# One global order for a decoder layer: the same instructions put out along one table over all engines

## The chip, the cores and the metric

The kernel runs on one core of one Trainium2 chip. The metric is the device time of one execution in microseconds; the median of three runs before the change is 768.79 us (768.78 to 768.81). A core has a tensor engine (PE) for matmuls, a vector engine (DVE), a scalar engine (ACT), GpSimd (POOL) and a sync engine (SP) that here only issues transfers. Each engine takes its instructions in the order in which they stand in its queue; semaphores hold an instruction until what it needs is there.

## The reference, cut to what matters

The layer has 512 tokens of width 1024. Three gated branches read the same normed input; two norms of the result and a feed-forward network (FFN) of width 2816 follow.

```python
u = rms_norm(h, ln_mix_pre[l])
qa, ka, va, qb, kb, vb, qm, gl = jnp.split(jnp.einsum('bsd,de->bse', u, w_in[l]), split_idx, axis=-1)
y_swa = swa_sink_attention(qa, ka, va, swa_sinks[l], rel_bias)   # 8 heads of 64, window 128
y_sb  = stick_breaking_attention(qb, kb, vb)                     # 8 heads of 64, causal
y_mem = memory_cross_attention(qm, mk, mv)                       # 4 heads of 128, memory of 256
g = jax.nn.sigmoid(gl.reshape(B, S, N_BRANCH, D))
merged = (g[:, :, 0] * (y_swa @ w_branch_swa) + g[:, :, 1] * (y_sb @ w_branch_sb)
          + g[:, :, 2] * (y_mem @ w_branch_mem))
h = h + rms_norm(merged @ w_out[l], ln_mix_post[l])
u = rms_norm(h, ln_ffn_pre[l])
h = h + rms_norm((jax.nn.silu(u @ w_gate[l]) * (u @ w_up[l])) @ w_down[l], ln_ffn_post[l])
```

(The heads' reshapes are left out here, and the einsums of the branches are written as products.)

## The kernel before

**Arithmetic.** All large products are f32 made of three float32r matmuls. ACT makes `hi`, a float32r copy of a tile (CAST in the profile), DVE makes `lo = raw - hi` (TENSOR_TENSOR `lo<-raw,hi`), and PE does hi by hi, hi by lo and lo by hi (`mm3`). Weights come in pieces of 128 by 1024 into four places `raw`, and are split into four places `hi` and four `lo`. The gate and branch products and the FFN are computed as seven products of half-size blocks in place of eight, with sums and differences on DVE.

**Stages by time.** From 0 to about 90 us the projections of the three attentions, with the mean square of x (`rstd_of`) and of the memory; from 90 to about 225 us stick-breaking and window attention, with the memory's attention and parts of the gates between; to about 370 us gates and branch products; then the product with `w_out`, the second norm, and from about 450 us the FFN, the last of it `w_down` and the output.

**The reciprocal root of x.** `rstd_of("x", ...)` sums squares over the partitions with two matmuls against ones (`sh_x` and `sl_x` are the two halves of the sum of squares); `rsqrt` then does Ln on ACT (`t_x<-bank,eps_t`), Exp on ACT (`wide<-t_x`), and one Newton step of three DVE instructions (`t_x<-wide`, `t_x<-t_x,v_x`, `wide<-t_x,wide`). Only with it can DVE empty the banks of the projections of keys and queries (`kb<-bank,wide`, `qb<-bank,wide`). `table(name)` asks for a table of functions on ACT (ACT_TABLE_LOAD in the profile); the first such call stands ahead of the first activation. `eps_t` is one column filled by a DVE MEMSET.

**Value products of 64 columns.** `sb_out` multiplies the attention weights of two heads (`at`) by the values (in `wide`), for key blocks 3, 2, 1 and 0, with 512, 384, 256 and 128 elements; the inner loop runs over the two heads, whose results lie in the two halves of one PSUM bank. These are plain f32 matmuls with 64 columns of weights. The window attention does the same with `pts`, 256, 256, 256 and 128 elements. Transposes go through PE against the identity `c_ident`.

**Order and places.** Every engine is wrapped by `Noted`, which calls the real engine at once and keeps the instruction (its call is line 232, so nearly all instructions bear that line in the profile). The program is thus put out in the order of the code. At the end of `tile_kernel` a table of five lists, one for each engine, gives the order that each engine is to keep: `follow` ties each instruction to the one ahead of it in its list. The lists are independent of each other. `Places` hands out the places of tiles by a second table, `PLAN`, in the order in which the code asks for them. Helpers for runs without tables (`after`, `behind`, `high_priority`) stand in the code as well.

Of the kernel before, what the change touches and what calls it, by code (L numbers as in the profile page):

```python
# [17 lines left out]
P = 128  # L18
# [19 lines left out]
ORDER = {  # L38
    "tensor": (
# [23 lines left out]
    ),  # L63
    "vector": (
# [81 lines left out]
    ),  # L146
}
PLAN = {
    "raw": (
# [2042 lines left out]
```

## Time and profile before

| what | value |
|---|---|
| median of 3 runs | 768.79 us (768.78 to 768.81) |
| span of the profiled execution, first to last instruction | 766.9 us |
| granted clock of PE, mean | 0.997 |
| PE busy | 759.1 us, 99%, 4073 matmul records |
| DVE busy | 675.2 us, 88%, 1100 |
| ACT busy | 520.3 us, 68%, 946 |
| POOL busy | 104.1 us, 14%, 140 |
| moved by DMA | 150.06 MB, mean 196 GB/s |

For the profiled execution the span alone is recorded; the median stands 1.9 us above it, which lies ahead of the first and behind the last instruction.

How rows of a timeline are read: start in us, duration in us, engine, line, operation, `out<-in` by the program's names with their numbers left out, partitions by elements, type, and how many instructions of one kind stand in the row; in brackets the idle time ahead and what ended it. For a matmul `128*64 128x512` means weights of 128 rows and 64 columns and a moving operand of 128 partitions by 512 elements. The record of a matmul includes its way through the array, so consecutive records overlap; the pitch from start to start is what a matmul costs in a row of them. Rows by stage give the stretch, its length, and then for PE, PE's weight loads, DVE, ACT and POOL the busy time with the count of instructions; behind them the clock, the DMA share and GB/s. A row of a group gives the busy time, the mean ns of one, and the idle time ahead with what ended it.

### The profile page before, as it was taken

Reading aid. Unit: us, or ns where it says so; the run is one execution under the profiler, and the core shown is the slowest. Engines: PE = TensorE matmul, PEld = TensorE weight load, DVE = VectorE, ACT = ScalarE, POOL = GpSimd, SP = SyncE. Lnnn points to the kernel's source line nnn. Section 1 sums busy time; section 2 is a strip of 40 time slices with the busy share of each in tenths; the row PEclk is TensorE's granted clock in tenths of the full one; section 3 lists DMA queues with packets and bytes.
Section 4 is the critical chain, followed back from the end, with each engine's and each line's share of the span. In section 5 each row is a group of like instructions: output and inputs, shape, how many; then the busy total and the mean of one; then the engine's idle time right before and its main releaser. Section 6 shows DMA issues by size and latency. Waiting matters only on the chain.

```text
span 766.9 us, 11497 instructions
## 1 busy us (share of the span) xinstructions
PE 759.1 (99%) x4073; PEld 647.3 (84%) x4073; DVE 675.2 (88%) x1100; ACT 520.3 (68%) x946; POOL 104.1 (14%) x140
## 2 busy tenths in 40 slices
PE   9999999999999999999999999999999999999996
PEld 6789888778888888888888899988888888888885
DVE  7994897799989756999897799899999999999966
ACT  7662677777997758677944596566666668957552
POOL 0303242000222110010001201100000000214000
PEclk9999999999999999999999999999999999999998
DMA  8548999734799895469949958876777746859922
GB/s 277 166 142 233 332 328 254 211 111 149 185 188 192 184 203 163 112 134 210 340 128 329 209 130 240 203 191 180 204 192 203 220 142 187 171 120 216 261 75 111
DMA packets 50170, 150.06 MB, mean 196 GB/s; under 512 B 5984, under 2 KB 7952, under 8 KB 50016
## 3 DMA queue, kind: packets, MB, share of 16 engines
q1 hardware_dynamic: 34224, 94.38, 36.8%
q0 software_dynamic: 15600, 54.80, 36.1%
q8 instruction: 32, 0.52, 0.3%
q14 instruction: 26, 0.21, 0.1%
q10 hardware_dynamic: 288, 0.13, 0.1%
HBM read 140.38 MB, written 19.40 MB: 208 GB/s over the span
## 4 chain that ended last, share of the span: by engine, by line
PE 96%; DMA 1%; DVE 1%; ACT 1%; issue 0%; SPq 0%; DVEq 0%
PE bank L232 96%; DMA xT<-in_xT 1%; DMA raw<-in_w_p 0%; DVE xacc L232 0%; SPq L232 0%; ACT pair L232 0%; DVE pair L232 0%; ACT hi L232 0%; ACT xT L232 0%; DVE lo L232 0%; DVE fg L232 0%; DVE sl_x L232 0%; DVEq L2180 0%; DVE s L232 0%; ACT sqr L232 0%
## 5 line engine op out<-in xcount | busy, mean ns | idle before, releaser
L232 PE MATMUL bank<-pair,hi 128*128 128x512 f32 (+1 forms) x1008 | 254.4, 368 | 0.0
L232 DVE TENSOR_TENSOR lo<-raw,hi 128x1024 fp32r<-128x1024 f32 (+4 forms) x149 | 170.7, 1149 | 36.8 <-ACT hi L232 36.2
L232 PEld LDWEIGHTS bank<-pair,hi 128*128 128x128 f32 x1008 | 177.5, 189 | 27.0 <-ACT hi L232 0.9
L232 ACT CAST hi<-raw 128x1024 fp32r<-128x1024 f32 (+4 forms) x149 | 147.7, 998 | 73.7 <-PE bank L232 54.5
L232 PE MATMUL bank<-hi,pair 128*128 128x512 f32 (+1 forms) x628 | 196.3, 374 | 0.0
L232 PE MATMUL bank<-pair,lo 128*128 128x256 f32 (+1 forms) x752 | 154.7, 302 | 0.0
L232 PEld LDWEIGHTS bank<-hi,pair 128*128 128x128 f32 x628 | 115.3, 188 | 19.5 <-issue 0.2
L232 PEld LDWEIGHTS bank<-pair,lo 128*128 128x128 f32 x752 | 115.6, 190 | 10.9 <-DVE lo L232 0.7
L232 PE MATMUL bank<-lo,pair 128*128 128x512 f32 (+1 forms) x330 | 123.6, 375 | 0.0
L232 ACT CAST hi<-wide 128x1024 fp32r<-128x1024 f32 (+1 forms) x61 | 62.2, 1024 | 27.0 <-PE bank L232 11.3
L232 DVE TENSOR_TENSOR lo<-wide,hi 128x1024 fp32r<-128x1024 f32 (+1 forms) x61 | 71.9, 1185 | 4.6 <-ACT hi L232 4.3
L232 PEld LDWEIGHTS bank<-lo,pair 128*128 128x128 f32 x330 | 62.0, 188 | 10.1
L232 POOL DMA_DIRECT2D raw<-in_w_g x24 | 21.1, 878 | 124.4 <-DVE lo L232 106.2
L232 DVE TENSOR_TENSOR gp<-gp,bank 128x512 f32<-128x512 f32 x49 | 33.6, 687 | 4.6 <-PE bank L232 3.7
L232 ACT ACTIVATE sg<-gp 128x256 f32<-128x256 f32 x42 | 17.7, 421 | 23.0 <-DVE gp L232 22.9
L232 POOL DMA_DIRECT2D raw<-in_w_gu x15 | 13.2, 924 | 147.6 <-DMA raw<-in_w_gu 138.5
L232 ACT COPY gp<-bank 128x512 f32<-128x512 f32 x42 | 24.7, 588 | 2.1 <-DVE aq L232 1.4
L232 DVE TENSOR_TENSOR_SCAN bw<-br,bw 128x512 f32<-128x512 f32 (+3 forms) x32 | 24.6, 809 | 0.2
L232 DVE TENSOR_TENSOR gp<-gp,hp 128x512 f32<-128x512 f32 x36 | 24.7, 685 | 0.0
L232 POOL DMA_DIRECT2D wide<-in_w_gu x12 | 11.2, 934 | 84.6 <-DMA wide<-in_w_gu 76.3
L232 ACT COPY hp<-bank 128x512 f32<-128x512 f32 x36 | 21.5, 598 | 0.0
L232 PE MATMUL bank<-hi,ll 128*128 128x512 f32 x50 | 19.4, 389 | 0.0
(624 smaller groups left out, 1371.8 us busy)
## 6 DMA issues: line engine op xcount, KB each, us to landing
wide<-in_w_gu SPq DMA_DIRECT2D x31, 512.0 KB, 5.1
raw<-in_w_gu SPq DMA_DIRECT2D x26, 512.0 KB, 5.4
raw<-in_w_g POOLq DMA_DIRECT2D x24, 512.0 KB, 6.0
raw<-in_w_g SPq DMA_DIRECT2D x18, 512.0 KB, 4.2
raw<-in_w_gu POOLq DMA_DIRECT2D x15, 512.0 KB, 7.2
raw<-in_w_p SPq DMA_DIRECT2D x14, 512.0 KB, 6.3
wide<-in_w_gu POOLq DMA_DIRECT2D x12, 512.0 KB, 5.8
raw<-in_w_brt SPq DMA_DIRECT2D x9, 512.0 KB, 4.8
```

What stands on the lines that cost most here:

```text
L232: ins = f(*args, **kw)
```

## The change

All calls to engines are first noted as `Op` in a `Program`: nothing is put out, and nothing is allocated. Tiles out of `PLAN` that need an allocation are `View`s made `once`, when the first instruction that uses them is put out. At the end one table `ORDER` over all 6328 operations (4009 for PE, 1068 for DVE, 876 for ACT, 136 for POOL, 239 for SP, the same operations in the same noted order as before) says in which order they are put out; each is tied to the one ahead of it on its own engine. Both tables are new: of PE's 4009 operations 2996 keep their order among themselves, of DVE's 1068 546, of ACT's 876 420, of POOL's 136 94 and of SP's 239 141. `PLAN` gives other places to the tiles. The helpers for runs without tables are gone. The only order that is still asserted is that an activation comes behind the call for its table.

```diff
-ORDER = {
-    "tensor": (
-        "0-18 21 19-20 22-24 27 25-26 28-529 538-561 572-575 580-588 642 562-564 566-567 576-579 530-537 613-620 569 "
...
-class Noted:
...
-            ins = f(*args, **kw)
-            self.seen.append(ins)
-            return ins
+ORDER = (
+    "3 1 13 630 15 18 4 12 632 263 16 5 17 631 6 19 267 7 20 299 21 8 23 37 9 303 25 38 10 22 335 39-40 11 26 339 "
...
+class Program:
+    def __init__(self):
+        self.ops = []
+
+    def put_out(self, nc, order, follow):
+        real = lambda x: x.real() if isinstance(x, View) else x
+        last, out = {}, set()
+        for n in order or range(len(self.ops)):
+            op = self.ops[n]
+            assert all(b.at in out for b in op.behind)
+            out.add(n)
+            args = [real(x) for x in op.args]
+            ins = getattr(getattr(nc, op.engine), op.name)(*args, **{k: real(x) for k, x in op.kw.items()})
+            if op.engine in last:
+                follow(ins, last[op.engine])
+            last[op.engine] = ins
...
 class Places:
...
         if kind == "ck" and n < SINGLES:
-            return pool.tile(shape, dt, tag=f"ck{n}", name=name, bufs=1)
+            return View(once(lambda: pool.tile(shape, dt, tag=f"ck{n}", name=name, bufs=1)))
...
     def table(name):
         ins = nc.scalar.preload_act_table_set(name)
-        for x in since:
-            after(ins, x)
+        ins.behind = tuple(since)
         since.clear()
         pin[:] = [ins]
...
     go(len(fs.units))
-    for e, text in ORDER.items():
-        seen, last = getattr(nc, e).seen, None
-        for part in text.split():
-            a, _, b = part.partition("-")
-            for k in range(int(a), int(b or a) + 1):
-                if last is not None:
-                    follow(seen[k], seen[last])
-                last = k
+    order = []
+    for part in ORDER.split():
+        a, _, b = part.partition("-")
+        order += range(int(a), int(b or a) + 1)
+    program.put_out(tc.nc, order, follow)
```

Three places show what moves. The rows give the line (232 before, 425 after, both the helper), the operation, and the tiles by name and number.

PE before, the first value products of stick-breaking attention, heads 0 and 1 (`at0...` and `at1...`); `mh` and `hi` behind them belong to the memory's keys:

```order
L232 MATMUL bank0_104<-kbs11_326,qbl11_456 128x256
L232 MATMUL bank0_104<-at10_1039,wide0_84 64x512
L232 MATMUL bank0_104<-at00_951,wide0_84 64x512
L232 MATMUL bank0_104<-at11_1040,wide0_84 64x384
L232 MATMUL bank0_104<-at01_952,wide0_84 64x384
L232 MATMUL bank0_104<-at12_1041,wide0_84 64x256
L232 MATMUL bank0_104<-at02_953,wide0_84 64x256
L232 MATMUL bank0_104<-at12_1041,wide0_84 64x128
L232 MATMUL bank0_104<-at02_953,wide0_84 64x128
L232 MATMUL bank0_104<-mh0_734,hi0_76 128x256
```

All eight groups of such products stand like this before. PE after, the third group, heads 4 and 5:

```order
L425 MATMUL bank0_101<-pair5_107,hi3_79 128x512
L425 MATMUL bank0_101<-at50_1447,wide0_84 64x512
L425 MATMUL bank0_101<-hi2_78,ml3_516 128x512
```
```order
L425 MATMUL bank0_101<-pair8_110,hi3_79 128x512
L425 MATMUL bank0_101<-at40_1404,wide0_84 64x512
L425 MATMUL bank0_101<-at51_1451,wide0_84 64x384
L425 MATMUL bank0_101<-at41_1392,wide0_84 64x384
L425 MATMUL bank0_101<-at52_1438,wide0_84 64x256
L425 MATMUL bank0_101<-c_ident_118,bw60_1455 128x128
L425 MATMUL bank0_101<-at42_1388,wide0_84 64x256
L425 MATMUL bank0_101<-at52_1438,wide0_84 64x128
L425 MATMUL bank0_101<-at42_1388,wide0_84 64x128
L425 MATMUL bank0_101<-pair2_104,pair3_105 128x512
```

`at50` now stands some ten matmuls ahead of its partner `at40`, and a transpose stands inside the rest. The 64 products stand in 20 unbroken runs in place of 8; the sizes of the runs are 1 and 7 (heads 0 and 1), 2, 3, 1 and 2 (2 and 3), 1, 4 and 3 (4 and 5), 2, 4 and 2 (6 and 7); then for the window's four pairs 7 and 1, 8, 5 and 3, and 1, 4 and 3. Transposes against `c_ident` stand in 57 runs in place of 42.

ACT before, around the root of x (`t_x` is Ln, `wide<-t_x` is Exp; its first table load is the third row of its queue, far ahead of these):

```order
L232 CAST sh_x_298<-xacc_203 128x512
L232 CAST hi0_76<-raw0_72 128x1024
L232 CAST hi1_77<-raw1_73 128x1024
L232 ACTIVATE t_x_305<-bank0_104,eps_t_119 128x512
L232 CAST hi2_78<-raw2_74 128x1024
L232 ACTIVATE wide0_84<-t_x_305 128x512
L232 CAST hi3_79<-raw3_75 128x1024
L232 CAST kbs00_316<-kb0_295 64x512
```

ACT after, the same place (`pair13<-xacc` is what `sh_x` was):

```order
L425 CAST pair13_115<-xacc_191 128x512
L425 CAST hi0_76<-raw1_73 128x1024
L425 CAST hi2_78<-raw2_74 128x1024
L425 CAST hi1_77<-raw0_72 128x1024
L425 CAST hi3_79<-raw3_75 128x1024
L425 CAST hi0_76<-raw1_73 128x960
L425 ACTIVATE mh0_431<-mT0_254,wide0_84 128x256
L425 ACT_TABLE_LOAD
L425 ACTIVATE t_x_440<-bank0_101,eps_t_116 128x512
L425 ACT_TABLE_LOAD
L425 ACTIVATE wide0_84<-t_x_440 128x512
```

Ln and Exp now come behind three more CASTs, and a table load stands ahead of each. In the table the call for the combined table comes behind both; the loads are put in as the program is built, which has 12 of them in place of 9. DVE after, the same place:

```order
L425 TENSOR_TENSOR lo3_83<-raw3_75,hi3_79 128x1024
L425 TENSOR_TENSOR lo0_80<-raw1_73,hi0_76 128x960
L425 MEMSET eps_t_116 128x1
L425 SCALAR_TENSOR_TENSOR t_x_440<-wide0_84 128x512
L425 SCALAR_TENSOR_TENSOR ml0_456<-mT0_254,wide0_84,mh0_431 128x256
L425 TENSOR_TENSOR t_x_440<-t_x_440,v_x_356 128x512
L425 SCALAR_TENSOR_TENSOR wide0_84<-t_x_440,wide0_84 128x512
L425 SCALAR_TENSOR_TENSOR ml1_472<-mT1_269,wide0_84,mh1_463 128x256
L425 SCALAR_TENSOR_TENSOR kb1_476<-bank0_101,wide0_84 128x512
L425 SCALAR_TENSOR_TENSOR kb2_482<-bank0_101,wide0_84 128x512
L425 SCALAR_TENSOR_TENSOR kb3_489<-bank0_101,wide0_84 128x512
```

The MEMSET of `eps_t` was the fourth instruction of DVE's queue before. It now stands behind the `lo0` of 960 elements, and `kb3` is the last of the first three banks that are emptied.

More of the change, by code (lines that the diff above doesn't have):

```diff
@@ new lines, with __init__, then, __getitem__ @@
+class View:
+    def __init__(self, make, path=(), shape=None):
+        self.make, self.path, self.shape = make, path, shape
+    def then(self, f):
+        return View(self.make, self.path + (f,))
+    def __getitem__(self, k):
+        return self.then(lambda ap: ap[k])
+    def bitcast(self, dt):
+        return self.then(lambda ap: ap.bitcast(dt))
+    def rearrange(self, *args, **kw):
+        return self.then(lambda ap: ap.rearrange(*args, **kw))
+    def unsqueeze(self, axis):
+        return self.then(lambda ap: ap.unsqueeze(axis))
+    def to_broadcast(self, shape):
+        return self.then(lambda ap: ap.to_broadcast(shape))
+    def real(self):
+        ap = self.make()
+        for f in self.path:
+            ap = f(ap)
+        return ap
@@ new lines, with __init__ @@
+class Op:
+    def __init__(self, at, engine, name, args, kw):
+        self.at, self.engine, self.name, self.args, self.kw = at, engine, name, args, kw
+        self.behind = ()
+class Program:
[13 more added lines that the diff above has]
+            last[op.engine] = ins
+        assert len(out) == len(self.ops)
@@ L256, in __getitem__, with once, f @@
         return self.held[c]
+def once(make):
+    got = []
+    def f():
+        if not got:
+            got.append(make())
+        return got[0]
+    return f
 class Places:
@@ L425, in split @@
         ins = nc.scalar.copy(hi, raw)
-        lows = nc.vector.tensor_tensor(lo, raw, hi.bitcast(F32), op=ALU.subtract)
-        if "behind" in st:
-            after(ins, st["behind"][0])
-            after(lows, st["behind"][1])
+        nc.vector.tensor_tensor(lo, raw, hi.bitcast(F32), op=ALU.subtract)
         return ins
@@ L456, in mm3 @@
         (lh, ll), (rh, rl) = l, r
-        one = nc.tensor.matmul(out, lh, rh, start=start, stop=False, skip_group_check=True)
+        nc.tensor.matmul(out, lh, rh, start=start, stop=False, skip_group_check=True)
         nc.tensor.matmul(out, lh, rl, start=False, stop=False, skip_group_check=True)
-        return one, nc.tensor.matmul(out, ll, rh, start=False, stop=stop, skip_group_check=True)
-    def mm3_behind(*args):
-        one, last = mm3(*args)
-        if "products" in st:
-            after(one, st["products"])
-        st["products"] = last
+        nc.tensor.matmul(out, ll, rh, start=False, stop=stop, skip_group_check=True)
     def mm(out, l, r, start, stop):
@@ L474, in tile_kernel @@
     pin, since = [], []
-    def after(ins, first):
-        if not ORDER:
-            follow(ins, first)
     def follow(ins, first):
@@ L486, in fn @@
         ins = nc.scalar.activation(*args, **kw)
-        for p in pin:
-            after(ins, p)
+        ins.behind = tuple(pin)
         since.append(ins)
@@ L971, in gen @@
                 for k in range(2):
-                    mm3_behind(sbank[i][:, :], seven_left(b, p, k, i), cols((hi, lo), k * 512, 512), first and k == 0, last and k == 1)
+                    mm3(sbank[i][:, :], seven_left(b, p, k, i), cols((hi, lo), k * 512, 512), first and k == 0, last and k == 1)
                 yield 1.36
@@ L1154, in first_split @@
         split(raws[i][:, sl], his[i][:, sl], los[i][:, sl])
-    with nullcontext() if ORDER else tc.manual_schedule():
-        idle = tc.nc.const_aps.tensor(1.0, [P, 512], BF16)
-        one_t = {}
-        for name in ("x", "m"):
-            one_t[name] = ck(f"on_{name}", F32R)[:, :P]
-            nc.vector.tensor_copy(one_t[name], idle[:, :P])
-        pw = dps("warm")
-        for i in range(WARM):
-            mm(pw[:, :], idle[:, :P], idle[:, :], True, True)
-        first_load(nc.scalar, 0, (0, 2))
-        first_table = nc.scalar.preload_act_table_set("natural_log_exp_and_others")
-        load_x(0, 1)
-        first_load(nc.sync, 0, (1,))
-        load_x(1, 2)
-        first_load(nc.sync, 1, (0, 1))
-        load_x(2, 3)
-        first_load(nc.sync, 1, (2,))
-        first_load(nc.sync, 2, (0,))
-        load_x(3, 4)
-        first_load(nc.sync, 2, (1, 2))
-        load_x(4, 5)
-        first_load(nc.sync, 3)
-        load_x(5, 8)
-        dn.loaded = dn.have = FIRST
-        for p in range(len(PIECE)):
-            for i in range(FIRST):
-                first_split(i, p)
-            for k in range(*PIECE[p]):
-                gain_split(k)
-        xacc = ck("xacc")
-        nc.scalar.activation(xacc[:, :], xraw[0][:, :], AF.Square)
-        for k in range(1, KC):
-            nc.scalar.activation(xraw[k][:, :], xraw[k][:, :], AF.Square)
-            nc.vector.tensor_tensor(xacc[:, :], xacc[:, :], xraw[k][:, :], op=ALU.add)
-        dn.ahead(4, 3)
-        for i in range(FIRST):
-            first_ps[("kb", i)] = aps(f"kb{i}")
-        order = [(i, 0, x) for x in ("hh", "lh", "hl") for i in range(FIRST)]
-        order += [(i, 1, x) for i in range(FIRST) for x in ("hh", "lh", "hl")]
-        for i, k, x in order:
-            w = (his if x[0] == "h" else los)[i]
-            mm(first_ps[("kb", i)][:, :], w[:, k * P : (k + 1) * P], u[k][x[1] == "l"], k == 0 and x == "hh", False)
-        gens = [dn.units[i]["mm"](his[i], los[i]) for i in range(FIRST)]
-        for k in range(2, KC + 1):
-            for g in gens:
-                next(g, None)
-        dn.at = FIRST
-        st["rs"], st["rb"] = rstd_of("x", xacc, S, aps)
-        st["chain"] = since[-1]
-        for f in st.pop("waiting"):
-            f()
@@ new lines, in tile_kernel @@
+    idle = tc.nc.const_aps.tensor(1.0, [P, 512], BF16)
+    one_t = {}
+    for name in ("x", "m"):
+        one_t[name] = ck(f"on_{name}", F32R)[:, :P]
+        nc.vector.tensor_copy(one_t[name], idle[:, :P])
+    pw = dps("warm")
+    for i in range(WARM):
+        mm(pw[:, :], idle[:, :P], idle[:, :], True, True)
+    first_load(nc.scalar, 0, (0, 2))
+    first_table = nc.scalar.preload_act_table_set("natural_log_exp_and_others")
+    load_x(0, 1)
+    first_load(nc.sync, 0, (1,))
+    load_x(1, 2)
@@ new lines, in tile_kernel @@
+    first_load(nc.sync, 1, (0, 1))
+    load_x(2, 3)
+    first_load(nc.sync, 1, (2,))
+    first_load(nc.sync, 2, (0,))
+    load_x(3, 4)
+    first_load(nc.sync, 2, (1, 2))
+    load_x(4, 5)
+    first_load(nc.sync, 3)
+    load_x(5, 8)
+    dn.loaded = dn.have = FIRST
+    for p in range(len(PIECE)):
+        for i in range(FIRST):
+            first_split(i, p)
+        for k in range(*PIECE[p]):
+            gain_split(k)
+    xacc = ck("xacc")
+    nc.scalar.activation(xacc[:, :], xraw[0][:, :], AF.Square)
@@ new lines, in tile_kernel @@
+    for k in range(1, KC):
+        nc.scalar.activation(xraw[k][:, :], xraw[k][:, :], AF.Square)
+        nc.vector.tensor_tensor(xacc[:, :], xacc[:, :], xraw[k][:, :], op=ALU.add)
+    dn.ahead(4, 3)
+    for i in range(FIRST):
+        first_ps[("kb", i)] = aps(f"kb{i}")
+    order = [(i, 0, x) for x in ("hh", "lh", "hl") for i in range(FIRST)]
+    order += [(i, 1, x) for i in range(FIRST) for x in ("hh", "lh", "hl")]
+    for i, k, x in order:
+        w = (his if x[0] == "h" else los)[i]
+        mm(first_ps[("kb", i)][:, :], w[:, k * P : (k + 1) * P], u[k][x[1] == "l"], k == 0 and x == "hh", False)
@@ L1210, in tile_kernel @@
+    gens = [dn.units[i]["mm"](his[i], los[i]) for i in range(FIRST)]
+    for k in range(2, KC + 1):
+        for g in gens:
+            next(g, None)
+    dn.at = FIRST
+    st["rs"], st["rb"] = rstd_of("x", xacc, S, aps)
+    for f in st.pop("waiting"):
+        f()
     pin[:] = [first_table]
     ident = const("ident", [P, P], base)
-    sinks = places.fixed(cst, [P, 8], F32, "sinks")
+    sinks = places.fixed([P, 8], "sinks")
     nc.sync.dma_start(sinks[:, :], a["sinks"].to_broadcast([P, 8]))
@@ L1401, in swa_pair @@
             pts[h] = [ck(f"pts{h}{i}") for i in range(2)]
-            with tc.high_priority():
-                nc.vector.tensor_copy(pts[h][0][:, P:], pt[h][0][:, P:])
-                nc.scalar.copy(pts[h][1][:, :], pt[h][1][:, :])
+            nc.vector.tensor_copy(pts[h][0][:, P:], pt[h][0][:, P:])
+            nc.scalar.copy(pts[h][1][:, :], pt[h][1][:, :])
         yield 2.0
@@ L2065, in tile_kernel @@
     kept(1)
-    behind(since[-1], st["mixed"])
     table("silu_and_others")
@@ L2071, in tile_kernel @@
     go(3)
-    behind(*turn(3, tmp[3]))
+    turn(3, tmp[3])
     fs.hold = 5
@@ L2075, in tile_kernel @@
     turn_n2(2)
-    behind(*turn_n2(3))
+    turn_n2(3)
     fs.hold = 6
@@ L2079, in tile_kernel @@
     turn_n22(2)
-    behind(*turn_n22(3))
+    turn_n22(3)
     fs.hold = 8
@@ L2083, in tile_kernel @@
     for t in (2, 3):
-        late = turn_late(t, 0)
-    behind(*late)
+        turn_late(t, 0)
     fs.hold = 10
```

263 lines of the change are left out of this document (108 added, 155 removed), and 424 rows, old and new, of tables (ORDER, PLAN).

## The prediction

> **What bounds the kernel now.** I read the page's first part, then the chain of waits, the tensor engine's waits, and busy time by stage.
>
> ```profile
> PE 759.1 (99%) x4073; PEld 647.3 (84%) x4073; DVE 675.2 (88%) x1100; ACT 520.3 (68%) x946; POOL 104.1 (14%) x140
> ```
> ```profile
> 22.29 737.97 PE bank L232 x3990
> 760.29 0.03 ACT sqr L232
> ```
> ```profile
> PE bank L232 <- PEq L2174: 0.8, 1, 0.8
> PE bank L232 <- DVE sl_x L232: 0.4, 1, 0.4
> ```
> ```profile
> 640.00:680.00 40.00, 40.00 (x200) 34.01 (x199) 39.74 (x55) 34.44 (x57) 5.31 (x6) 1.00 0.76 184
> 680.00:720.00 40.00, 40.00 (x179) 33.10 (x178) 39.88 (x61) 26.62 (x42) 12.30 (x14) 1.00 0.98 216
> ```
>
> From 22.29 us on the chain is one piece of 738 us on the tensor engine (PE); it waits 1.2 us in all, 0.8 of that before its first instruction. A new order can therefore gain only what PE wastes by its own order: 0.4 us of waiting, and a little between forms. It can lose in two ways: PE's order may cost more time for the same matmuls, or another engine may come late. The last fence shows where the second is close: in the FFN the vector engine (DVE, third pair) is busy 39.74 and 39.88 of 40 us. Nothing is added or removed in arithmetic, so every term is one of order.
>
> **The change, part by part.** The sum is made against the profiled span, 766.9 us, which stands 1.9 below the median of 768.79; I add 1.9 at the end.
>
> **A. Torn pairs (64-column products).** The value products of stick-breaking (`at`) and window attention (`pts`) are plain f32 and use 64 of the array's 128 columns, one head left, the next right. Before, all 64 stand in eight unbroken groups of eight, heads alternating.
>
> ```profile
> 108.85 0.28 PE L232 MATMUL bank<-kbs,qbl 128*128 128x256 f32 x1
> 109.05 2.38 PE L232 MATMUL bank<-at,wide 128*64 128x512 f32 x16
> 111.36 0.39 PE L232 MATMUL bank<-mh,hi 128*128 128x256 f32 x1
> 111.58 0.28 PE L232 MATMUL bank<-ml,hi 128*128 128x256 f32 x1
> 111.70 0.27 PE L232 MATMUL bank<-mh,lo 128*128 128x256 f32 x1
> ```
> ```profile
> L232 PE MATMUL bank<-at,wide 128*64 128x384 f32 x16 | 3.3, 486 | 0.0
> L232 PE MATMUL bank<-at,wide 128*64 128x256 f32 x16 | 2.4, 379 | 0.0
> ```
>
> Each such matmul leaves two records (x16 for eight). By the second fence 128 more elements make a record 107 ns longer, 0.836 ns per element, so a matmul alone would take 2 x 0.836 = 1.67 ns per element. The group has 2 x (512+384+256+128) = 2560 elements: 4.28 us one after the other. It took 109.05 to 111.36, 2.31 us: half of 4.28 (2.14) plus 0.17. So the two heads run side by side, and a half without its partner pays the whole.
>
> In the new table the 64 stand in 20 runs. A run takes the longer of its two heads' sums. For heads 4 and 5: `at50` (512) alone; then 896 for `at40`, `at41` against 640 for `at51`, `at52`; then 384 against 128: 512+896+384 = 1792 instead of 1280, 512 extra. The eight groups give 512, 256, 512, 0, 128, 0, 256, 256 extra: 1920 x 1.67 ns = **+3.2 us**. Strict pairing, where a half overlaps only its neighbour, gives 2432 and 4.1; if a lone half found its partner across what stands between, 0. I take 3.2, since inside a run the heads still alternate.
>
> Each run also has edges: the entry, 108.85 to 109.05, is 0.20 and the exit, 111.36 to 111.58, is 0.22, where the usual step of a 256-element matmul is 0.12 (111.58 to 111.70): +0.08 and +0.10; and inside 0.17. That is 0.35 per run; 12 more runs are **+4.2 us**, between 0 (if the edges belong to the pairing and a short run has none) and 4.2. I take the row. That exit also shows that what follows does not run alongside.
>
> The Trainium skill, page TensorEngine Tiling (Array Packing), section Key Properties, says that a change of tiling mode drains the TensorE and that tiles work independently. That speaks against this change and agrees with 0.35 and with the halving; it has no price, so the sum by it is the same.
>
> **B. Transposes torn from their runs.** Those through `c_ident` stand in 57 runs, before in 42.
>
> ```profile
> 97.93 0.39 PE L232 MATMUL bank<-pair,lo 128*128 128x512 f32 x1
> 98.16 1.25 PE L232 MATMUL bank<-c_ident,bw 128*128 128x128 f32 x10
> 99.17 0.48 PE L232 MATMUL bank<-kbs,qbs 128*128 128x512 f32 x1
> 99.48 0.39 PE L232 MATMUL bank<-kbs,qbl 128*128 128x512 f32 x1
> ```
>
> Ten take 98.16 to 99.17, 1.01, less than 10 x 0.107; the matmul behind takes 0.31 to the next, 0.08 over the usual 0.23. Together about 0.03 per run: 15 x 0.03 = **+0.5 us**, bounds 0 and 15 x 0.08 = 1.2.
>
> **C. The rstd of x.** Before, the logarithm's table is loaded ahead of the first activation, and Ln and Exp follow with none between. Now that load stands behind Exp in the order, so the built program has one ahead of Ln and one between Ln and Exp. Ln also needs `eps_t`, whose MEMSET has moved on DVE behind a `lo0` of 960 elements; its `hi0` waits until PE has read the former `hi0`.
>
> ```profile
> 39.70 0.62 PE L232 MATMUL bank<-pair,hi 128*128 128x512 f32 x2
> ...
> 40.38 0.62 PE L232 MATMUL bank<-pair,hi 128*128 128x512 f32 x2
> ```
> ```profile
> 22.96 0.68 ACT L232 ACTIVATE t_x<-bank,eps_t 128x512 f32<-128x512 f32 x1
> 23.54 1.03 ACT L232 CAST hi<-raw 128x1024 fp32r<-128x1024 f32 x1
> 24.48 0.63 ACT L232 ACTIVATE wide<-t_x 128x512 f32<-128x512 f32 x1
> ...
> 33.63 1.00 ACT L232 CAST hi<-raw 128x960 fp32r<-128x960 f32 x1
> ...
> 81.60 0.42 ACT L232 ACTIVATE wide<-t_m 128x256 f32<-128x256 f32 x1
> 82.03 1.28 ACT L232 ACT_TABLE_LOAD   x1
> 83.33 0.98 ACT L232 ACTIVATE br<-bank 128x512 f32<-128x512 f32 x2
> ```
> ```profile
> 27.87 0.69 DVE L232 SCALAR_TENSOR_TENSOR wide<-t_x,wide 128x512 f32<-128x512 f32 x1
> 28.60 0.69 DVE L232 SCALAR_TENSOR_TENSOR kb<-bank,wide 128x512 f32<-128x512 f32 x1
> ...
> 35.01 1.15 DVE L232 TENSOR_TENSOR lo<-raw,hi 128x960 fp32r<-128x960 f32 x1
> ...
> 53.93 0.48 DVE L232 SCALAR_TENSOR_TENSOR ml<-mT,wide,mh 128x256 fp32r<-128x256 f32 x1
> ```
>
> PE's pace is three matmuls in 0.68 (39.70 to 40.38), 0.227 each. From `sl_x` (22.29, now some 0.4 earlier) to the last reader of the old `hi0` are 47 of them: 32.6. Then `hi0` on the scalar engine (ACT) 32.9 to 33.9, `lo0` on DVE to 35.1, `eps_t` 35.2. ACT: load 1.28, begun after a short `mh0`, to 35.6; Ln 0.68, 36.3; load 1.28, 37.6; Exp 0.63, 38.2. DVE: three operations like that at 27.87, 0.69 to 0.73 each, with `ml0` (0.48) between, 40.8; `ml1` 0.48; `kb1`, `kb2`, `kb3` at 0.69: 43.3. Meanwhile PE does 41 matmuls from 32.6 and at 41.9 wants the bank that `kb3` empties: 1.5 late. Behind Exp, ACT has `mh3`, `mh2` and `mh1`, the memory's halves, whose products PE does only much later. Behind `kb3` in DVE's queue are `kb0` and `qb0`, 44.7, where PE, shifted, would come at 44.3: 0.4; then 0.2 for `qb2`. **+2.1 us**; bounds 0 (without the two loads it just fits) and 4, if DVE's queue runs late by as much again. Before, rstd was ready at 28.6 (the `kb` row), and that was the cover.
>
> The Trainium skill, page ScalarE: Activation LUTs, section Table sets: the hidden batching unit, lets a logarithm and the exponential behind it share one load through the combined set; the same page prices a switch at about 2.66 us with its drain. The row differs: 82.03 follows 81.60 + 0.42, and the next starts at 83.33, so 1.28 to 1.31 is all. By the page the chain would end 2 x 1.38 later and the sum would be an estimated 2.8 higher.
>
> **D. Start, tail, waiting.** At the start ACT now puts one 128-element CAST ahead of the first `pair` and a 256-element one ahead of the next 128s:
>
> ```profile
> 4.00 0.51 ACT L232 ACTIVATE pair<-wide 128x256 fp32r<-128x256 f32 x1 [1.05 <-DMA wide<-in_xg]
> 4.41 0.68 ACT L232 CAST hi<-raw 128x128 fp32r<-128x128 f32 x3
> ```
>
> 0.23 (a third of 0.68) and about 0.3: **+0.5 us**, bounds 0 and 1 (the third raw piece now stands seventh in SP's queue). At the end `fg31` is done before `fg30`, and the output DMAs go out interleaved: **+0.2**, bounds 0 and 0.7. Two matmuls now stand between `sh_x` and `sl_x`, filling the 0.4 wait: **-0.4**.
>
> **E. DVE in the FFN.** The sums per stage are alike in both orders, 37 more DVE instructions wait for a semaphore, and its slack of 0.12 to 0.26 in 40 us is the cover. I take 0. Without cover:
>
> ```profile
> L232 DVE TENSOR_TENSOR lo<-raw,hi 128x1024 fp32r<-128x1024 f32 (+4 forms) x149 | 170.7, 1149 | 36.8 <-ACT hi L232 36.2
> ```
>
> 36.8 idle over 149 is 0.25 per waiting instruction; 37 x 0.25 = 9.1, the upper bound.
>
> Sum: 3.2 + 4.2 + 0.5 + 2.1 + 0.5 + 0.2 - 0.4 = +10.3. 766.9 + 10.3 + 1.9 = **779.1 us**.
>
> **The rivals.**
> 1. *Cheaper*: edges are free and the rstd chain is hidden. 10.3 - 4.2 - 2.1 = +4.0: **772.8**. For it: C misses its cover by only 1.5 us; against: both groups' edges stand in rows.
> 2. *DVE becomes the bound*: up to 9.1 on top, **784 to 788**, taking effect once the 0.38 us of slack from 640 to 720 is used. For it: 39.88 of 40. Against: PE slowed by 7 us earlier gives DVE a head start there.
> 3. *Halves find each other*: PE holds the lone half open until its partner comes, A vanishes: 779.1 - 7.4 = **771.7**. Against: the exit at 111.36, behind which nothing runs alongside.
> 4. *Not slower*: DVE, not PE, sets the FFN's pace, so that PE's matmuls there are stretched by late operands, and the new table relieves it by work done ahead of 640. To come out level it must give back the 10.3 of A to D, an eighth of these 80 us: **about 769**, or below. It decides if PE's pitch there is above 0.227. Against: 40 us for 179 matmuls is 0.223, PE's own pace.
> 5. *Dear loads*: each load empties ACT as the page says, 2.8 more by that bound's mechanism: **782**. Against: 83.33.
>
> **How the numbers follow.** Forecast, 776 to 783: 0.60. Rival 1 (772 to 776): 0.13. Rival 2: 0.12. Rival 3: 0.04. Rival 4: 0.06. Rival 5: 0.05, inside the forecast's range. A measurement of this kernel tells about 0.2%, 1.5 us, from no change: faster is below 767.3, slower above 770.3. Rival 4 is split between faster (0.03) and same (0.03), with 0.01 of rivals 1 and 3 in same: faster 0.03, same 0.04, slower 0.93. The range 773 to 788 leaves out rivals 3 and 4, a third of 1 and the far end of 2: under 2 in 10.
>
> **What would show it.** A: lone `at` and `pts` matmuls with a pitch of 1.67 ns per element, and about 7 us more for the 64, edges included, between 90 and 225. B: nothing large. C: two loads of 1.28 around Ln near 35 us, and a wait of PE for DVE `kb` near 42. D: the first real matmul near 5.2. E: no waits of PE for DVE `lo` after 450. Wrong would be: runs of one `at` that cost no more than half, or a PE idle by more than 2 us in the FFN.

## The result and the profile after

| kernel | median us | ratio to before (95% interval) | span of the profile |
|---|---|---|---|
| before | 768.78 (768.58 to 768.81) | | 766.9 |
| changed | 820.83 (819.68 to 821.15) | 1.0676 (1.0661 to 1.0691) | 818.9 |

The change costs 52 us. 779.1 was forecast, with a range up to 788: the direction was right, the size was not.

The page's first part of the changed kernel, busy time and share of the span by engine:

```profile
PE 783.2 (96%) x4073; PEld 645.4 (79%) x4073; DVE 677.9 (83%) x1100; ACT 527.1 (64%) x949; POOL 107.2 (13%) x140
```

DVE and ACT have as much work as before (677.9 and 527.1 us, against 675.2 and 520.3). PE now stands idle for 36 us, where it was 8. What PE waits for in the changed kernel (us in total, times, longest):

```profile
PE bank L425 <- ACT hp L425: 18.8, 30, 0.7
PE bank L425 <- ACT yq L425: 2.5, 6, 0.6
PE bank L425 <- ACT hi L425: 1.0, 1, 1.0
PE bank L425 <- DVE kb L425: 0.9, 1, 0.9
...
PE bank L425 <- ACT sg L425: 0.8, 2, 0.5
```

Thirty waits for one kind of ACT instruction are new, and all lie in the FFN. By stage (PE, weight loads, DVE, ACT, POOL):

```profile
540.00:580.00 40.00, 35.22 (x193) 29.76 (x192) 33.80 (x45) 22.39 (x33) 3.50 (x4) 1.00 0.66 155
740.00:780.00 40.00, 40.00 (x178) 33.10 (x178) 35.84 (x58) 26.81 (x46) 9.71 (x11) 1.00 0.84 190
```

From 540 to 580 no engine is full: PE is idle 4.8 of 40 us, DVE 6.2, ACT 17.6. That is no engine that has fallen behind, but engines that wait for each other. From 740 on PE is full again. One such place, PE of the changed kernel:

```profile
548.57 1.54 PE L425 MATMUL bank<-pair,hi 128*128 128x512 f32 x6
549.95 0.40 PE L425 MATMUL bank<-pair,lo 128*128 128x256 f32 x2
551.02 0.61 PE L425 MATMUL bank<-pair,lo 128*128 128x256 f32 x3 [0.68 <-ACT hp L425]
551.47 0.40 PE L425 MATMUL bank<-pair,hi 128*128 128x512 f32 x1
```

ACT at the same place:

```profile
550.38 0.59 ACT L425 COPY hp<-bank 128x512 f32<-128x512 f32 x1 [1.02 <-PE bank L425]
550.86 1.05 ACT L425 CAST hi<-raw 128x1024 fp32r<-128x1024 f32 x1
```

PE stops after two matmuls of the `lo` half of a product; ACT has waited for exactly these, copies, and PE goes on 0.05 us after the copy ends. Two matmuls of 256 elements at 0.12 us would have let the third begin at 550.19; it began at 551.02, 0.83 late, and these three took 0.45 where 0.36 is usual. So this stop costs 0.92 us; thirty like it would be 27.6, which is an estimate from this one place. At the like place before, PE runs through (first fence) while ACT empties the bank of a product that is done (second):

```profile
523.10 1.11 PE L232 MATMUL bank<-pair,lo 128*128 128x256 f32 x8
524.05 2.00 PE L232 MATMUL bank<-pair,hi 128*128 128x512 f32 x8
```
```profile
524.63 0.59 ACT L232 COPY gp<-bank 128x512 f32<-128x512 f32 x1
525.10 0.61 ACT L232 COPY hp<-bank 128x512 f32<-128x512 f32 x1
```

The code tells why. A wide product of the FFN lies in two banks; each holds the main half (`gp`, elements 0 to 255) and the rest (`hp`, 256 to 511). The rest is complete after the eight `hi` matmuls; the `lo` matmuls go on in the main half of the same banks. Before, the program was put out as the code notes it, product first, then both copies, and the per-engine lists did not alter who waits for whom: `hp` waited for the whole product. In the changed kernel the place in the one table also decides who waits. There 31 copies `hp` stand between the `lo` matmuls of their product, 8 copies `yq` in the attention's products, 2 `sg` and 2 score reads likewise: 43 readers of a bank into which PE is still writing. The program makes PE's later matmuls come behind each of them, and PE's list above shows 38 of the 43 as waits (30 for `hp`, 6 for `yq`, 2 for `sg`). Before has none.

### The profile page after: what moved, and what is told of

The parts are those of the page before. It is cut to its first block, busy times and chain, and to the rows that moved or that the text cites. A ratio compares the mean times of both kernels' runs of the same rounds, so it can differ in the third digit from the quotient of the medians.

```text
span 818.9 us, 11567 instructions
## 1 busy us (share of the span) xinstructions
PE 783.2 (96%) x4073; PEld 645.4 (79%) x4073; DVE 677.9 (83%) x1100; ACT 527.1 (64%) x949; POOL 107.2 (13%) x140
## 4 chain that ended last, share of the span: by engine, by line
PE 87%; ACT 6%; DVE 3%; DMA 1%; issue 1%; DVEq 0%; ACTq 0%
PE bank L425 87%; ACT hp L425 2%; DMA raw<-in_w_g 1%; DVE lo L425 1%; ACT hi L425 1%; ACT yq L425 0%; ACT L425 0%; DVE fg L425 0%; DMA raw<-in_w_p 0%; DVE gp L425 0%; ACT pair L425 0%; DVE s L425 0%; DVE kb L425 0%; ACT sqr L425 0%; DVE t_x L425 0%
## 5 line engine op out<-in xcount | busy, mean ns | idle before, releaser
L425 PE MATMUL bank<-hi,pair 128*128 128x512 f32 (+1 forms) x734 | 222.3, 378 | 1.1 <-ACT hi L425 1.0
L425 DVE TENSOR_TENSOR lo<-raw,hi 128x1024 fp32r<-128x1024 f32 (+4 forms) x155 | 176.9, 1151 | 44.1 <-ACT hi L425 38.3
L425 ACT CAST hi<-raw 128x1024 fp32r<-128x1024 f32 (+4 forms) x155 | 152.9, 995 | 79.3 <-PE bank L425 53.2
L425 PE MATMUL bank<-pair,lo 128*128 128x256 f32 (+1 forms) x752 | 164.7, 306 | 19.6 <-ACT hp L425 18.8
L425 PEld LDWEIGHTS bank<-hi,pair 128*128 128x128 f32 x734 | 134.6, 188 | 28.9 <-ACT hi L425 2.3
L425 PE MATMUL bank<-lo,pair 128*128 128x512 f32 (+1 forms) x372 | 137.2, 377 | 0.8 <-DVE lo L425 0.8
L425 PEld LDWEIGHTS bank<-lo,pair 128*128 128x128 f32 x372 | 69.5, 188 | 14.1 <-DVE lo L425 1.7
L425 DVE TENSOR_TENSOR lo<-wide,hi 128x1024 fp32r<-128x1024 f32 (+1 forms) x55 | 64.8, 1183 | 14.4 <-ACT hi L425 9.6
L425 ACT CAST hi<-wide 128x1024 fp32r<-128x1024 f32 (+1 forms) x55 | 56.0, 1021 | 26.8 <-PE bank L425 20.9
L425 PE MATMUL bank<-pair,pair 128*128 128x512 f32 (+2 forms) x112 | 32.2, 371 | 0.0
```

Of the source, the lines that this page charges most:

```text
L425: ins = getattr(getattr(nc, op.engine), op.name)(*args, **{k: real(x) for k, x in op.kw.items()})
```

## The experiments

The edits are made in the tables. A number is an operation by its place in the notes.

**1. The FFN's copies behind their product.** 4435 is one `hp`, 4426 to 4433 are the `lo` matmuls of its product.

```diff
-    "... 4426 4427 4435 4428 4386 4429 4430 4441 4364 4439 4431 4432 4409 4433 4442 ..."
+    "... 4426 4427 4428 4386 4429 4430 4441 4364 4439 4431 4432 4409 4433 4435 4442 ..."
```

> The changed kernel; in its table the 31 ACT copies hp<-bank of the FFN, which stand between the matmuls of the product whose bank they read, are put out behind that product's last matmul. The tensor engine's order is not touched, 22 of ACT's instructions move. Theory 1 (a copy of a bank's finished half that is put out inside the product makes the later matmuls of the same bank wait for it): 31 waits of 0.84 us and 0.10 us at the matmul behind each go, about -29 us, so near 792 us (790 to 795), and the waits of PE for ACT hp are gone. Theory 2 (ACT and DVE are late in the FFN by themselves, and hp is only where it shows; the prediction's rival 2): the next wait takes its place, not more than 10 us are won, 811 us or more.

Measured: 798.42 us (798.24 to 799.28), ratio 1.039 (1.0374 to 1.0405): 22.4 us of 52 come back. PE's waits in this run:

```profile
PE bank L413 <- ACT yq L413: 2.5, 6, 0.6
PE bank L413 <- ACT hi L413: 1.7, 2, 1.2
PE bank L413 <- ACT gp L413: 1.6, 6, 0.4
PE bank L413 <- ACT pair L413: 1.0, 2, 0.6
```

`hp` is gone from the list, though PE's order is untouched. That is far beyond theory 2's 10 us, but 6 short of theory 1: `gp`, which ACT copies next to `hp`, is now waited for six times, and `hi` longer.

**2. All 43 behind their product.** 1245 is one `yq`, 1239 to 1241 are the last matmuls of its product.

```diff
-    "... 1238 1245 1258 1239 1240 1241 1271 ..."
+    "... 1238 1258 1239 1240 1241 1245 1271 ..."
```

> As the run before, and also the 8 copies yq<-bank of the attention, 2 activations sg<-bank and 2 score reads w<-bank that stand inside their product are put out behind it. Theory 1: the waits of PE for yq (4.5 us with those that wait for pts as well) and for sg (1.1 us) go too, about 6 us below the run before, near 786 us. Theory 2: no difference to the run before beyond 1 us.

Measured: 795.13 us (794.01 to 796.32), ratio 1.0345 (1.0329 to 1.036). 3.3 us below the first run, between the two theories: the waits for `yq` and `sg` went, about half of their time did.

**3. The tables of before in the new code.** Both tables are replaced; the order is that in which the instructions of before began in its profile.

```diff
 ORDER = (
-    "3 1 13 630 15 18 4 12 632 263 16 5 17 631 6 19 267 7 20 299 21 8 23 37 9 303 25 38 10 22 335 39-40 11 26 339 "
+    "263 12 15 1 3 2 4 13 16 639 5 17 14 0 6 18 7 19 8 20 9-10 39-40 11 21 33 41 22 35 93 37 74 23 94 34 95 36 24 "
...
```

> The changed kernel's code with the tables of before: the places of before, and one order over all engines that is the order in which the instructions of before began in its profile; each engine's own order is that of before, and no copy stands inside its product. Theory 1 (only the new table's numbers cost time): 768.8 us as before, within 0.2%. Theory 3 (putting out along one table, with places given when put out, costs by itself, by more or other waits): over 772 us.

Measured: 768.63 us (768.48 to 768.97), ratio 1.0001 (0.9992 to 1.001). The way of putting out costs nothing. All 52 us are in the numbers of the tables.

**4. The early copies alone, on the tables of before.**

```diff
-    "... 4428 4429 4409 4430 4431 4432 4433 4441 4415 4434 4442 4443 4435 4444 ..."
+    "... 4428 4429 4409 4435 4430 4431 4432 4433 4441 4415 4434 4442 4443 4444 ..."
```

> The run before (tables of before in one order), with the 31 ACT copies hp<-bank of the FFN put out as early as the new table does, after the first matmuls of the lo half of their product; 30 then stand inside it. The tensor engine's order stays that of before. Theory 1: 30 waits of 0.8 to 0.95 us each, 24 to 29 us above the run before, 793 to 798 us, with PE waiting for ACT hp about 30 times. Theory 2 (only a late ACT or DVE makes it wait): ACT has time here, less than 5 us above, under 774 us.

Measured: 803.27 us (802.88 to 803.8), ratio 1.0453 (1.0435 to 1.047). 34.6 us, more than theory 1 allowed, for moving 31 of ACT's copies by some ten places, 30 of them into their product, and nothing else. PE's waits, and one place on PE and on ACT:

```profile
PE bank L402 <- ACT hp L402: 27.0, 30, 1.4
```
```profile
527.62 0.63 PE L402 MATMUL bank<-pair,lo 128*128 128x256 f32 x4
529.40 0.75 PE L402 MATMUL bank<-pair,lo 128*128 128x256 f32 x4 [1.15 <-ACT hp L402]
```
```profile
527.82 1.05 ACT L402 CAST hi<-raw 128x1024 fp32r<-128x1024 f32 x1 [1.19 <-PE bank L402]
528.77 0.58 ACT L402 COPY hp<-bank 128x512 f32<-128x512 f32 x1
```

Here another instruction, a CAST of 1.05 us, stood on ACT ahead of the copy, and PE waited for both. Over the thirty stops the loss is 1.15 us each on average (34.6 / 30). ACT had time: it stood idle 1.19 us ahead of that CAST.

**5. The pairs of heads together again, in run 2's table.** The 64 matmuls are moved to where the last of their group of eight stood (1238 to 1241 end the group of heads 4 and 5). Seven groups become whole. In that of heads 4 and 5 the transpose 1258 still stands between `at50` (1234) and the other seven, so there are nine runs, not eight.

```diff
-    "... 1234 1202 1204 1218 ... 1235 860 1236 862 1208 1237 1224 1238 1258 1239 1240 1241 ..."
+    "... 1202 1204 1218 ... 860 862 1208 1224 1234 1200 1209 1258 1235 1236 1237 1238 1239 1240 1241 ..."
```

> The second run (all 43 copies put out behind their product, 795.1 us) with the 64-column matmuls of each pair of heads brought together again: eight groups of eight at the place where the last of each group stood. In that run's trace the 20 runs of them took 20.8 us against 16.0 for the eight of before, and their entries and exits about 0.19 us each more than usual. Theory 1 (the torn pairs cost what the prediction's term A says, 7.4 us, now read as 4.9 + 12 x 0.19 = 7.1): 788 us (787 to 789). Theory 2 (other engines are late anyway and the time won turns into waits): 792 us or more.

Measured: 796.74 us (795.37 to 798.0), ratio 1.036 (1.0345 to 1.0375): nothing is won. PE's waits in this run, and one place:

```profile
PE bank L412 <- DVE bw L412: 2.1, 1, 2.1
PE bank L412 <- DVE mk L412: 2.1, 2, 1.8
```
```profile
147.13 1.07 PE L412 MATMUL bank<-at,wide 128*64 128x512 f32 x2
150.29 0.33 PE L412 MATMUL bank<-c_ident,bw 128*128 128x128 f32 x1 [2.08 <-DVE bw L412]
150.55 2.37 PE L412 MATMUL bank<-at,wide 128*64 128x512 f32 x14
```

By the number theory 2 holds. The products themselves did get cheaper: without the two waits that lie inside or just behind their runs (1.8 and 2.1 us) they take 17.0 us where run 2 had 20.8, and PE's busy time falls from 776.8 to 773.4 us. But PE reaches the memory's products and the transposes sooner and waits for DVE instead. One of these waits is the edit's own work: in run 2 four products of heads 4 and 5, 1.65 us, stood ahead of the transpose 1258 and covered a part of its wait; here they stand behind it. So the run shows that time won on PE turned into waits, and not that a better place for the pairs would win nothing.

**6. And the table load and eps_t first.**

```diff
-    "3 1 13 630 15 18 4 12 632 263 ... 352 309 353 14 392 ... 285 0 169 ..."
+    "3 1 14 0 13 630 15 18 4 12 632 263 ... 352 309 353 392 ... 285 169 ..."
```

> The run before with the call for the combined function table put first on ACT and the MEMSET of eps_t first on DVE, as before the change. Theory 1 (the root of x comes late because of two table loads and eps_t): the wait of PE for DVE kb, 0.9 us idle and 1.05 with the matmul behind it, and the 0.2 behind it go, 1.2 to 1.5 us below the run before, near 786.6; the prediction said 2.1. Rival: kb is late by DVE's order and not by the table, under 0.4 us.

Measured: 795.65 us (794.71 to 796.55), ratio 1.0352 (1.0338 to 1.0367), 1.1 below the run before, but the two spreads overlap. In the trace PE no longer waits for `kb`; the time alone would not have shown it. PE still waits for `bw` as in run 5, and here something else comes behind it (the last row is a row by stage for PE alone: its busy time, the clock, the DMA share and GB/s):

```profile
147.30 0.47 PE L412 MATMUL bank<-c_ident,bw 128*128 128x128 f32 x1 [2.07 <-DVE bw L412]
147.70 3.85 PE L412 MATMUL bank<-at,wide 128*64 128x512 f32 x14
```
```profile
147.30:150.70 3.40, 3.40 (x11) 0.50 0.96 251
```

The same seven products took 2.37 us in run 5 and take 3.85 here, because the granted clock is 0.50 for 3.4 us from the end of the wait on: some 1.7 us lost. Run 5 has one such stretch, from 111.77 to 115.18, 1 us behind its wait of 1.8 us for `mk`, and run 8 one of 6.8 us among waits of 1.3, 0.8 and 1.5 us. The other profiled executions have none between start and end. Not each long wait does it: the one of 2.08 us in run 5 does not, and what decides is not shown.

**7. The pairs torn, on the tables of before.** The runs of the new table, with three matmuls between; one copy of ACT out of a bank of these products moves with them.

```diff
-    "... 1234 1205 1208 1235 1210 1236 1237 1238 1211 1239 1240 1241 1212 ..."
+    "... 1221 800 1247 1248 1235 1236 1237 1238 1166 1249 1250 1251 1239 1240 1241 ..."
```

> The tables of before in one order (768.6 us), with the eight groups of 64-column matmuls torn into the 20 runs of the new table, three other matmuls between two runs; 30 of the tensor engine's matmuls move, nothing else, and no copy stands inside a product. Theory 1 (a run takes its longer head and each run has edges of 0.35 us): 1920 elements x 1.67 ns and 12 x 0.35, 7.1 to 7.4 us above, 775.7 to 776.1. Theory 2 (lone halves overlap what stands beside them): 770 us or less.

Measured: 777.03 us (776.62 to 777.13), ratio 1.0109 (1.0095 to 1.0124): 8.4 us. A lone half in this run:

```profile
144.02 1.07 PE L401 MATMUL bank<-at,wide 128*64 128x512 f32 x2
145.03 0.73 PE L401 MATMUL bank<-pair,hi 128*128 128x512 f32 x2
145.59 0.40 PE L401 MATMUL bank<-pair,lo 128*128 128x512 f32 x1
```

512 elements took 144.02 to 145.03, 1.01 us: 512 x 1.67 ns is 0.855, and about 0.15 beside it. 145.03 to 145.59 is 0.56 for two matmuls that usually take 0.45: 0.11 for the exit. The rule of the longer head with its edges holds as it was forecast. PE also waited 0.9 us once for a `yq` that came later; that is the rest of the 8.4, and why the time lies just above the 776.1 of theory 1.

**8. ACT and DVE in another order, in run 6's table.** Operations are taken by when PE needs what comes of them.

```diff
 ORDER = (
-    "3 1 14 0 13 630 15 18 4 12 632 263 ..."
+    "1 13 630 15 632 0 18 12 639 263 3 16 2 37 631 33 4 267 14 17 5 19 299 6 20 303 7 21 8 335 23 9 25 339 10 22 "
...
```

> The run e4_all (copies behind, pairs whole, table first; 795.7 us), the tensor engine's, SP's and POOL's orders and all places as there, but ACT and DVE take their instructions in another order: by when the tensor engine needs what comes of them; 336 of ACT's and 403 of DVE's move. What is left there are some 30 waits of PE of 0.2 to 2.7 us for ACT and DVE, 12 us in rows, and what follows each. Theory 4 (ACT and DVE take the wrong work first): at least 10 us are won back, 785 us or less. Theory 5 (the tensor engine's order and the places give the operands no lead, whatever ACT and DVE take first): not more than 5 us, 790 us or more.

Measured: 808.45 us (807.11 to 813.46), ratio 1.053 (1.0489 to 1.0572). That is 12.8 us worse than run 6, with other waits in the place of the old ones:

```profile
PE bank L415 <- ACT pair L415: 4.4, 4, 1.8
PE bank L415 <- ACT gq2p L415: 2.5, 2, 1.8
```

By the number theory 5 stands, but the order was a worse one, so the run does not tell whether a better one would win the time back.

**9. The other twelve early readers, on the tables of before.**

```diff
-    "... 1211 1239 1240 1241 1212 ... 1253 1245 1254 ..."
+    "... 1211 1245 1239 1240 1241 ... 1253 1254 ..."
```

> The tables of before in one order (768.6 us), with the 8 copies yq<-bank, 2 activations sg<-bank and 2 score reads w<-bank outside the FFN's wide products put out as early as the new table does, inside their products; the tensor engine's order stays. Theory 1 (each such copy makes the matmuls behind it wait, as hp did in the FFN at 1.15 us each): 8 to 12 waits of 0.5 to 1.15 us, 4 to 13 us above, 773 to 782 us, with PE waiting for ACT yq. Theory 2 (it is something of the FFN's wide products alone): under 770 us.

Measured: 780.11 us (779.81 to 780.4), ratio 1.0149 (1.0134 to 1.0165): 11.5 us, 0.96 for each of the twelve. PE's waits:

```profile
PE bank L402 <- ACT yq L402: 3.8, 8, 0.6
PE bank L402 <- DVE s L402: 1.2, 2, 0.6
PE bank L402 <- ACT sg L402: 1.0, 2, 0.5
```

So it is nothing of the FFN alone. DVE's reads do it like ACT's: `s` is the second output of the two reads `w`.

**10. All three edits on the tables of before** (4, 7 and 9 together; the diffs are those).

> The tables of before in one order (768.6 us) with all three edits together: the 30 copies hp and the 12 others put out inside their products, and the 64-column pairs torn into the new table's 20 runs. Alone they cost 34.6, 11.5 and 8.4 us, 54.5 in all, where the whole change cost 52. Theory 6 (these three are what the change costs; what is still missing when they are taken out of the new table is lateness of ACT and DVE that lay under these waits): the costs add up here, since ACT and DVE have before's lead: 820 to 825 us, the changed kernel's 820.8 or just above. Rival (their costs overlap, and the new table has a further loss of its own beside them): 810 us or less.

Measured: 817.75 us (817.47 to 818.15), ratio 1.0643 (1.0626 to 1.0661): 49.1 us. They overlap by 5.4 of 54.5, so the number lies just below what theory 6 gave, and far above its rival. PE's waits look like those of the changed kernel:

```profile
PE bank L401 <- ACT hp L401: 27.3, 30, 1.4
PE bank L401 <- ACT yq L401: 2.6, 5, 0.6
```

49 of the 52 us are made again from before's tables by these three edits. Taken out of the new table, the copies gave back 25.7 us (run 2), and copies and pairs together 24.1 (run 5).

**11. The last two products: who reads the bank first.** 6316 is ACT's `sqr` of the last one, 6323 DVE's `fg`.

```diff
-    "... 6314 6315 6298 6316 6319 6318 6323 6320 ..."
+    "... 6314 6315 6298 6323 6316 6319 6318 6320 ..."
```

> The tables of before in one order (768.6 us); only the two last products of the FFN: DVE's read of the bank (fg) is put out ahead of ACT's read of the same bank (sqr), as the new table has it, before it was the other way round. The mean square of the row comes from sqr. Theory 1 (two readers of one bank are held apart as well, in the order in which they are put out): ACT starts sqr only behind DVE, 0.7 us later, 769.2 to 769.5 us, and the profile shows ACT waiting for DVE fg at the end. Theory 7 (two readers do not hinder each other): 768.6 us, and ACT waits for PE there.

Measured: 769.44 us (769.27 to 770.01), ratio 1.0011 (1.0002 to 1.002): 0.8 us above run 3. ACT in this run, in the changed kernel, and before:

```profile
761.10 0.60 ACT L403 ACTIVATE sqr<-bank 128x512 f32<-128x512 f32 x1 [2.53 <-DVE fg L403]
```
```profile
811.65 0.60 ACT L425 ACTIVATE sqr<-bank 128x512 f32<-128x512 f32 x1 [2.53 <-DVE fg L425]
```
```profile
760.29 0.60 ACT L232 ACTIVATE sqr<-bank 128x512 f32<-128x512 f32 x1 [2.15 <-PE bank L232]
```

Two readers of one bank are held apart too, and the one that the table puts first goes first.

## Why the prediction was wrong, point by point

**E, DVE in the FFN, is the step that failed.** It took 0, looked for cover on DVE alone, and made the upper bound 9.1 from 37 more waits of DVE. The waits that came were PE's, for ACT's copies out of a bank that PE was still filling: 27.6 us by an estimate from the rows of the changed kernel, 22.4 by taking them away (run 1), 34.6 by putting them in (run 4). The prediction asked how early an operand is ready; it did not ask what the one table does to the direction of a wait. Its list of what bounds the kernel had the clue: with PE hardly ever idle, an instruction of another engine that is ordered between two matmuls of one bank has no idle time of PE to fall into, and 38 of the 43 stopped it. The sign that the prediction itself gave for being wrong, a PE idle by more than 2 us in the FFN, came with 18.8 us for `hp` alone. Rival 2 put the loss in the right stage, but for a wrong cause: DVE was less busy in the FFN than before (33.80 and 35.84 of 40 us in the rows above, 39.74 and 39.88 in the prediction's).

The Trainium skill, page PSUM — Partial Sum Buffer, section PSUM bank collisions raise a hardware error, has the rule that was missed: PSUM is to be guarded by bank and quadrant of partitions and not by address, reads by ACT and DVE against each other included. The waits here agree: `hp` reads elements 256 to 511, the held matmuls write 0 to 255, and PE waits 0.68 us for it; and in run 11 ACT waits for DVE on two reads. What the hardware would do without these waits no run here shows.

**A, the torn pairs, was right.** Forecast +7.4, run 7 gives 8.4, of which 0.9 is a wait that was not in it. The changed kernel itself:

```profile
144.34 1.07 PE L425 MATMUL bank<-at,wide 128*64 128x512 f32 x2
145.34 0.50 PE L425 MATMUL bank<-hi,ml 128*128 128x512 f32 x1
...
147.97 1.72 PE L425 MATMUL bank<-at,wide 128*64 128x512 f32 x8
149.62 0.33 PE L425 MATMUL bank<-c_ident,bw 128*128 128x128 f32 x1
150.22 0.86 PE L425 MATMUL bank<-at,wide 128*64 128x256 f32 x6 [0.28 <-ACT yq L425]
```

The lone `at50` takes 1.00 us, and the four of the next run 1.65, which is 896 x 1.67 ns and 0.15. But that it adds to the sum independently of the rest is not borne out: taken out of the new table (run 5, all but one lone half), it gave nothing back, though that edit made a wait of its own. Rival 3, that halves find each other, is refuted by run 7.

**B, transposes,** forecast +0.5, was not measured by itself.

**C, the root of x, was right in its chain and too dear by 0.9.** ACT of the changed kernel, and PE behind it:

```profile
35.55 1.28 ACT L425 ACT_TABLE_LOAD   x1
36.84 0.69 ACT L425 ACTIVATE t_x<-bank,eps_t 128x512 f32<-128x512 f32 x1
37.55 1.28 ACT L425 ACT_TABLE_LOAD   x1
38.84 0.63 ACT L425 ACTIVATE wide<-t_x 128x512 f32<-128x512 f32 x1
```
```profile
42.99 0.39 PE L425 MATMUL bank<-pair,lo 128*128 128x512 f32 x1
44.27 0.70 PE L425 MATMUL bank<-pair,hi 128*128 128x512 f32 x2 [0.89 <-DVE kb L425]
```

Both loads, Ln and Exp stand where the chain had them, some 1.2 us later. PE came later too: 42.99 to 44.27 is 1.28 where 0.23 is usual, 1.05 lost against 1.5. Of the 0.6 behind it about 0.2 came. The loads took 1.28 and the next instruction followed at once, so rival 5's price does not show here either: the trace differs from the Trainium skill's page ScalarE: Activation LUTs, on which that price rested.

**D.** The first real matmul starts at 5.19 where it was 4.75: +0.44 for +0.5. The wait for `sl_x` is gone, as forecast. The tail was forecast at +0.2. From the start of the last matmul to the end of the span it is 8.8 us (810.12 to 818.9) where it was 7.1 (759.86 to 766.9): 1.7 more. The last `sqr` started 1.5 us behind the last matmul (810.12 to 811.65), and 0.4 behind it before (759.86 to 760.29). Run 11 has the same 1.5 (759.57 to 761.10) and costs 0.8 us, so about half of the 1.7 is the mechanism of E between two readers; the other half was not taken apart.

**The other rivals.** The cheaper one failed with both of its conditions: the edges are real, and `kb` was late. Not slower: PE's pitch in the FFN was its own, as said against it (740 to 780: 178 matmuls in 40 us, 0.225).

**What stays open.** With the copies behind their products, the pairs together but for one lone half and the load early, the new table still stands at 795.7, 27 us above before. By the pages its span is 27.9 us longer than before: 14.5 of that is idle time of PE (22.3 against 7.8 us), and 13.4 lies in time in which PE counts as busy (772.5 against 759.1). The waits in its list are many and small, 12.9 us in 21 waits for ACT and DVE; of the busy part the fall of the clock is 1.7, and the rest was not taken apart. That ACT and DVE were as late in the changed kernel and that this lay under PE's stops fits run 10 (the three edits alone make 49 of the 52 us when ACT and DVE keep before's lead) and run 5 (time won on PE turns into waits for DVE). But this is an argument and not shown. Whether it is the order of ACT and DVE, PE's own, or the places of the tiles that leaves the operands no lead is not settled: run 8 was meant to tell and does not.

## What to carry to other kernels

When instructions of several engines are put into one order, ask for each reader of a PSUM bank whether matmuls into that bank, at any address, still come behind it; such a reader stops a full tensor engine for a round trip, about 0.9 to 1.2 us here. A reader that could start early because its half is complete is best left behind the whole product. Costs that are seen when they are added to a good order need not come back when they are taken out of a bad one, so an account of a loss is made from both sides.

## What the runs showed of the hardware

- A stop of PE costs more than its idle time: at 551.02 it was idle 0.68, lost 0.83 to the next start, and 0.09 more on the three matmuls behind it.
- A 64-column f32 half without its partner costs 1.67 ns per element and about 0.15 us (512 elements: 1.01 us at 144.02 in run 7, 1.00 at 144.34 in the changed kernel); its exit costs 0.11 more.
- Behind or among waits of PE of 0.8 to 2.1 us the granted clock fell to 0.50 for 3.4 us (runs 5 and 6) and 6.8 us (run 8); the 3.4 us at 147.30 in run 6 cost some 1.7 us.
- Order alone, with the same work and the same engine order on PE, moved the kernel by 34.6 us (run 4).
